# A stick-breaking attention stage: high parts of a head pair's result one step ahead of their low parts, and earlier requests for the second head's first queries

## The chip, the core and the metric

The kernel runs on one core of one Trainium2 chip. Its engines work side by side, each through its own instructions in program order: TensorE (PE: matrix products; its weight loads are listed as PEld), VectorE (DVE), ScalarE (ACT), GpSimd (POOL), and SyncE (SP), which issues most of the transfers between memory (HBM) and the core's on-chip memory. The metric is the device time of one execution in microseconds (us), lower being better, as the median of several executions. A profile of one execution, taken apart from the timed ones, says when each instruction ran and what ended each engine's idle time.

## What is computed

One inference step of a one-layer streaming encoder on a prompt of 1024 frames, and on 32 sample frames behind a cache of 256. After a norm and one wide projection come three branches: attention with 8 heads of 64, a short convolution, and two gates. Then follow an output projection, a wide layer with a squared ReLU, an embedding branch and a final norm. The part around the change is the attention of the prompt:

```python
def stick_breaking(q, k, v, q_pos, k_pos):
    scale = 1.0 / math.sqrt(HEAD_DIM)
    z = jnp.einsum('bqhd,bkhd->bhqk', q.astype(jnp.float32), k.astype(jnp.float32)) * scale
    mask = k_pos[None, :] < q_pos[:, None]
    log_1m = jnp.where(mask, jax.nn.log_sigmoid(-z), 0.0)
    tail = lax.cumsum(log_1m, axis=3, reverse=True) - log_1m
    a = jnp.where(mask, jnp.exp(jax.nn.log_sigmoid(z) + tail), 0.0)
    out = jnp.einsum('bhqk,bkhd->bqhd', a, v.astype(jnp.float32))
    return out.astype(v.dtype)

# in layer(), with attend = stick_breaking swept over blocks of 128 queries:
    y_attn = attend(q, k, v).reshape(b, t, SB_WIDTH) @ w_attn_out
    conv_out, new_buf = causal_conv(cc * cx, conv_buf, conv_w)
    y_conv = (cb * conv_out) @ w_conv_out
    merged = jax.nn.sigmoid(ga) * y_attn + jax.nn.sigmoid(gc) * y_conv
```

All tensors are float32. For the products a float32 operand is written as a high part of lower precision and a low part, the rest; ACT makes the high part (a copy with a cast), DVE subtracts it to get the low part, and PE multiplies high by high, high by low and low by high.

## The kernel before

The program is one list of instructions for each engine. For PE, ACT, DVE and POOL it is written out by hand (`manual_schedule`), in the order in which the code calls them; the order of SP's transfers is made from the program's order and what they depend on. Completed transfers are counted by eight counters used in turn, so that on SP a transfer also waits for the one that was issued eight before it.

The attention of the prompt is a loop over 64 steps `(p, j, i)`: 4 head pairs p, the 2 heads j of a pair, and 8 blocks i of 128 queries; step n = 16 p + 8 j + i. At loop turn n these things are issued, by the letters of `ORDER`:

- `scores` (S) for step n: PE multiplies the block's queries by the keys (`z`, lines L1421 and L1422), ACT takes the sigmoid (`r`, L1423), POOL masks the diagonal block (L1430).
- `weigh` (L) for step n-1: a scan on DVE along the keys (`r`, L1437), the running product of the sticks. Behind it `settle_owed` adds the two halves of an earlier product into the pair's result `oT` (L1408, a DVE addition).
- `flip` (A and B) for step n-2: PE turns the weights (`pa`, L1473), ACT makes their high part and DVE the low part (`at`, L1476 and L1477).
- `gather` (G) for step n-3, after every second block: PE multiplies the turned weights by the values (`av`, L1492), and ACT moves one half out (`avl`, L1503).
- `fill` (F), between these: products of other stages, of the embedding (`ps_pw`) first and of the convolution branch (`ps_oc`) later, which keep PE busy.

Queries come in pieces of two blocks: `queries(p, j, c)` asks for one of four pieces of a head in three transfers (128, 64 and 64 KB, lines L1384 to L1386) into one of three buffers `Q`. The four pieces of the very first head have their own buffers and are asked for earlier. From turn 4 on, at each even turn, the piece of step n+4 is asked for. Keys and values of a head (`ks`, L1391, and `vv`, L1393) are asked for eight steps ahead, at the third block of the head before. Other transfers of that time are the sample's cache (`cv<-in_cache_v_dram`), an output of the embedding (`ed<-em`, 528 KB) and operands of the convolution.

When a head pair is done, `oT[p]` (128 x 1056) is split into `oh[p]` and `ol[p]` for the branch's output product. `branch_parts(p, c)` does half c of it: c=0 at the end of turn 16 (p+1) + 8, c=1 one turn later (`BP = (8, 9)`), that is at turns 24 and 25, 40 and 41, 56 and 57 for pairs 0 to 2, and after the loop for pair 3. Through `split_into` (L1509 and L1510) it issues the copy on ACT (`o0h` and so on) and at once the subtraction on DVE (`o0l`).

Of the kernel before, what the change touches and what calls it, by code (L numbers as in the profile page):

```python
# [9 lines left out]
F32 = mybir.dt.float32  # L10
# [65 lines left out]
def tile_step(  # L76
# [8 lines left out]
    nc = tc.nc  # L85
# [7 lines left out]
    def blk(name, dt=F32, shape=None):  # L93
        return bpool.tile(shape or [P, T], dt, tag="B", name=name)
# [55 lines left out]
    halves = [slice(0, TH), slice(TH, T)]  # L150
    quarters = [slice(t * TQ, (t + 1) * TQ) for t in range(4)]
    oper = {k: [None] * 4 for k in ("B11", "B12", "B21", "B22", "T1", "T2", "T3", "T4")}
    add, sub = ALU.add, ALU.subtract
    dve, pool = nc.vector.tensor_tensor, nc.gpsimd.tensor_tensor
# [876 lines left out]
    oT = []  # L1031
# [345 lines left out]
    def queries(p, j, c):  # L1377
        if (p, j) == (0, 0):
            q = blk(f"q{c}", F32R, [P, 2, 256])
        else:  # L1380
            q = apool.tile([P, 2, 256], F32R, tag="Q", name=f"q{p}{j}{c}", bufs=3)
        live["q", p, j, c] = q
        src = qd[p, 64 * j : 64 * j + 64, :, c * 256 : (c + 1) * 256]
        nc.sync.dma_start(q[0:64, :, :].bitcast(F32), src)  # L1384
        nc.sync.dma_start(q[64:128, 0, :].bitcast(F32), src[:, 1, :])
        nc.sync.dma_start(q[64:128, 1, :].bitcast(F32), src[:, 0, :])  # L1386

    def keys_values(p, j):
        kk = st["k", p, j] = blk(f"ks{p}{j}", F32R, [P, SEQ])
        for i in range(2):  # L1390
            nc.sync.dma_start(kk[64 * i : 64 * i + 64, :].bitcast(F32), kd[p, i, 64 * j : 64 * j + 64, :])  # L1391
        vv = st["v", p, j] = blk(f"vv{p}{j}", F32R, [P, 8, P])
        nc.sync.dma_start(vv.bitcast(F32).rearrange("p a c -> p (a c)"), vd[p, j])  # L1393

    def branch_parts(p, c):
        if c == 0:
            oh.append(blk(f"o{p}h", F32R))  # L1400
            ol.append(blk(f"o{p}l", F32R))
        split_into(oh[p], ol[p], oT[p], [halves[c]])

    owed = []

    def settle_owed():
        while owed:
            owed.pop(0)()  # L1408

    steps = [(p, j, i) for p in range(4) for j in range(2) for i in range(8)]  # L1410

    def scores(p, j, i):
        q, kk = live["q", p, j, i // 2], st["k", p, j]
        L = P * (i + 1)
        nh = 1 if L <= 512 else 2
        W = L // nh
        tq = slice((i % 2) * P, (i % 2) * P + P)
        r = apool.tile([P, SEQ], F32, tag="R", name=f"r{p}{j}{i}", bufs=4)
        for h in range(nh):
            z, c = zps.tile([P, 512], F32, tag="z", name=f"z{p}{j}{i}{h}")[:, :W], slice(h * W, h * W + W)  # L1420
            nc.tensor.matmul(z, q[:, 0, tq], kk[:, c], start=True, stop=False)  # L1421
            nc.tensor.matmul(z, q[:, 1, tq], kk[:, c], start=False, stop=True)  # L1422
            nc.scalar.activation(r[:, c], z, AF.Sigmoid, scale=-1.0)  # L1423
        earlier(r[:, L - P : L], 1.0)
        live[p, j, i] = (r, L)
# [18 lines left out]
    def weigh(p, j, i):  # L1444
        left_over(*live[p, j, i])
# [6 lines left out]
    def flip(p, j, i):  # L1452
        nm = f"{p}{j}{i}"
        s, L = live.pop((p, j, i))
        c, u = i // 2, i % 2
        if u == 0:
            live["A"] = [[None, None], [None, None]]
            for s_ in range(2):
                nblk = min(4, 2 * c + 2 - 4 * s_)
                if nblk <= 0:  # L1460
                    continue
                for hl in range(2):
                    if nblk == 4:
                        a = blk(f"at{nm}{hl}{s_}", F32R, [P, 4, 256])
                    else:
                        a = apool.tile([P, 2, 256], F32R, tag="A2", name=f"at{nm}{hl}{s_}", bufs=2)
                    live["A"][hl][s_] = a
        A = live["A"]
        for b0 in range(0, i + 1, 4):
            nb = min(4, i + 1 - b0)  # L1470
            pt = turned([P, 4, P], f"pa{nm}{b0}")
            for b in range(nb):
                nc.tensor.transpose(pt[:, b, :], s[:, (b0 + b) * P : (b0 + b + 1) * P], ident)  # L1473
            ah = A[0][b0 // 4][:, :nb, u * P : (u + 1) * P]
            al = A[1][b0 // 4][:, :nb, u * P : (u + 1) * P]
            nc.scalar.copy(ah, pt[:, :nb, :])  # L1476
            nc.vector.tensor_tensor(al, pt[:, :nb, :], ah.bitcast(F32), op=ALU.subtract)  # L1477
            if b0 == 0 and i >= 4:
                yield
        if u:  # L1480
            live["A", p, j, c] = A

    def gather(p, j, c):
        A = live.pop(("A", p, j, c))
        vv = st["v", p, j]
        av = turned([P, 256], f"av{p}{j}{c}")
        n = 2 * c + 2
        turns = [(b, hl) for b in range(n - 2) for hl in range(2)]
        turns += [(n - 2, 0), (n - 1, 0), (n - 1, 1), (n - 2, 1)]
        for k, (b, hl) in enumerate(turns):  # L1490
            q0 = P * (b == n - 1)
            nc.tensor.matmul(  # L1492
                av[:, q0:], vv[:, b, :], A[hl][b // 4][:, b % 4, q0:],
                start=k == 0, stop=k + 1 == len(turns),
            )
        if j == 0 and c == 0:
            oT.append(blk(f"oT{p}"))
        if j == 1 and c == 3:
            nc.scalar.copy(oT[p][:, SEQ:], osT[:, p, :])
        lo = tpool.tile([64, 256], F32, tag="avl", name=f"avl{p}{j}{c}", bufs=2)  # L1500
        for u in range(2):
            q = slice(u * P, u * P + P)
            nc.scalar.activation(lo[:, q], av[0:64, q], AF.Identity, bias=vend[:, p, 8 * j + 2 * c + u : 8 * j + 2 * c + u + 1])  # L1503
        owed.append(partial(dve, oT[p][64 * j : 64 * j + 64, c * 256 : (c + 1) * 256], av[64:128, :], lo, op=add))


    def split_into(h, l, src, parts):
        for c in parts:
            nc.scalar.copy(h[:, c], src[:, c])  # L1509
            nc.vector.tensor_tensor(l[:, c], src[:, c], h[:, c].bitcast(F32), op=ALU.subtract)  # L1510
# [8 lines left out]
    oh, ol, mg, mh, ml = [], [], [], [], []  # L1519
# [26 lines left out]
    def gates_load(n):  # L1546
        sg = merge_gates[n] = [blk(f"s{n}{i}") for i in range(2)]
        for i in range(2):
            nc.sync.dma_start(sg[i], gd[8 * i + n])

    def gates_ready(n):
        if n < RAW_GATES:
            sg = merge_gates[n][0]
            scaled(sg)
            nc.scalar.activation(sg, sg, AF.Sigmoid)
# [35 lines left out]
    def fill(upto):  # L1591

        nonlocal done
        while done < upto - 0.1:
            done += next(work, 1.0)
# [136 lines left out]
    with tc.manual_schedule(engines=MM):  # L1732
        next(sample)
        for n in range(len(steps) + LAG + 1):
            done_f, parts = 0, None
            w0, w1 = (pace_ + [FILL])[n : n + 2]
            if n < len(steps):
                i = steps[n][2]
                if i % 2 == 0 and 4 <= n < len(steps) - 4:
                    p_, j_, i_ = steps[n + 4]  # L1740
                    queries(p_, j_, i_ // 2)
                if i == 2 and n + 8 < len(steps):
                    keys_values(*steps[n + 8][:2])
            if n - 4 in (4, 6, 8, 11, 12, 13, 14):
                next(sample)

            for op in ORDER:
                if op == "S" and n < len(steps):
                    scores(*steps[n])
                elif op == "L":  # L1750
                    if 1 <= n <= len(steps):
                        weigh(*steps[n - 1])
                    settle_owed()
                elif op == "F":
                    done_f += 1
                    fill(START + w0 + (w1 - w0) * done_f / nf)
                elif op == "G" and n > LAG and steps[n - LAG - 1][2] % 2 == 1:
                    p, j, i_ = steps[n - LAG - 1]
                    gather(p, j, i_ // 2)
                elif op in "AB" and LAG <= n < len(steps) + LAG:  # L1760
                    if op == "A":
                        parts = flip(*steps[n - LAG])
                    next(parts, None)
            if n in range(*AT):
                next(sums_w, None)
            if 16 < n < 64 and n % 16 in BP:
                branch_parts(n // 16 - 1, BP.index(n % 16))
        settle_owed()
        branch_parts(3, 0)
        branch_parts(3, 1)  # L1770
        gates_load(0)
        gates_ready(0)
    c_att.close()
# [1017 lines left out]
```

## Time and profile before

| | us |
|---|---|
| median of 3 runs | 1508.69 |
| lowest and highest of them | 1507.28, 1509.08 |
| the profiled execution | 1510.69 |
| its span on the core | 1508.8 |

How to read the rows that follow. A row of the timeline gives start, duration, engine, line, operation, out<-in, shape and count; idle time of the engine ahead of it stands in brackets, with what ended it. SPq is the issuing of a transfer on SP's queue, not its way through the DMA engines; the list of transfers gives KB of one and us from issue to landing. A row of the list of waits gives the total, how often, and the longest. A row of a window gives its length, the busy time of PE, PEld, DVE, ACT and POOL with counts, then the granted clock of PE, the busy share of the DMA engines and their GB/s. Starts of matrix products are recorded, their ends are modelled.

### The profile page before, as it was taken

The numbers are of one execution on the slowest core, as the hardware profiler recorded it, in microseconds if no ns is written. First come the engines' busy times: TensorE is split into PE (matmuls) and PEld (weight loads), VectorE is DVE, ScalarE is ACT, GpSimd is POOL, SyncE is SP. The second block draws the span as 40 slices with busy tenths as digits, with TensorE's granted clock in tenths as the row PEclk, the third lists the DMA queues.
The fourth block names the chain that finished last, engine by engine and source line by source line (L and its number), as shares of the span: only waits on it lengthen the run. The fifth ranks groups of instructions, "written<-read, shape, count | busy, mean of one in ns | idle before, by whom it ended". The sixth has DMA issues, their size and how long they took to land.

```text
span 1508.8 us, 29621 instructions
## 1 busy us (share of the span) xinstructions
PE 1491.1 (99%) x11520; PEld 1476.0 (98%) x11520; DVE 1189.2 (79%) x1716; ACT 802.7 (53%) x1595; POOL 376.8 (25%) x326
## 2 busy tenths in 40 slices
PE   9999999999999999999999999999999999999997
PEld 9999999999999999999999999999999999999997
DVE  6867788879578999876788778888688878879766
ACT  7654444445467767433475555555655433334655
POOL 0434334444121222003323344344000000000251
PEclk9999999999999999999999999999999999999999
DMA  6624425422679666654647677766989757855443
GB/s 242 215 72 170 169 58 198 156 84 92 225 244 278 182 167 140 225 199 160 230 175 245 242 258 250 253 240 226 352 300 287 245 190 244 286 185 167 141 128 123
DMA packets 127773, 303.37 MB, mean 201 GB/s; under 512 B 14961, under 2 KB 35569, under 8 KB 127633
## 3 DMA queue, kind: packets, MB, share of 16 engines
q1 hardware_dynamic: 122512, 286.97, 56.1%
q0 software_dynamic: 1728, 6.29, 2.5%
q10 hardware_dynamic: 3392, 8.23, 1.6%
q8 instruction: 90, 1.47, 0.4%
q14 instruction: 51, 0.41, 0.1%
HBM read 219.89 MB, written 89.93 MB: 205 GB/s over the span
## 4 chain that ended last, share of the span: by engine, by line
PE 86%; DVE 6%; DMA 3%; ACT 3%; issue 1%; SPq 0%; ACTq 0%; DVEq 0%
PE ps_dn L2220 6%; PE ps_dn L2218 6%; PE ps_dn L2219 6%; PE ps_A11i L453 4%; PE ps_A11i L454 4%; PE ps_A11i L455 4%; PE ps_A11u L453 3%; PE ps_A11u L454 2%; PE ps_A11u L455 2%; PE av L1492 2%; PE ps_wo L133 2%; PE ps_wo L135 2%; PE ps_wo L134 2%; PE ps_S1i L455 2%; PE ps_S1i L454 2%; PE ps_S1i L453 2%
## 5 line engine op out<-in xcount | busy, mean ns | idle before, releaser
L2220 PE MATMUL ps_dn<-fhP,wlo_dn 128*128 128x264 f32 x768 | 218.5, 285 | 0.0
L2218 PE MATMUL ps_dn<-fhP,whi_dn 128*128 128x264 f32 x768 | 218.3, 284 | 0.0
L2219 PE MATMUL ps_dn<-flP,whi_dn 128*128 128x264 f32 x768 | 218.2, 284 | 0.0
L2220 PEld LDWEIGHTS ps_dn<-fhP,wlo_dn 128*128 128x128 f32 x768 | 144.5, 188 | 0.0
L2218 PEld LDWEIGHTS ps_dn<-fhP,whi_dn 128*128 128x128 f32 x768 | 144.5, 188 | 0.0
L2219 PEld LDWEIGHTS ps_dn<-flP,whi_dn 128*128 128x128 f32 x768 | 144.4, 188 | 0.0
L2433 POOL TENSOR_TENSOR xx<-xx,pgs 128x400 f32<-128x400 f32 (+1 forms) x17 | 20.1, 1184 | 280.3 <-DVE pgs L2432 279.8
L1437 DVE TENSOR_TENSOR_SCAN r<-r 128x128 f32<-128x128 f32 (+3 forms) x64 | 86.7, 1355 | 4.1 <-POOL r L1430 4.1
L453 PE MATMUL ps_A11i<-T,shS_i 128*128 128x264 f32 x288 | 82.4, 286 | 0.7 <-ACT u_i L596 0.7
L454 PE MATMUL ps_A11i<-T,shS_i 128*128 128x264 f32 x288 | 82.2, 285 | 0.0
L455 PE MATMUL ps_A11i<-T,slS_i 128*128 128x264 f32 x288 | 82.0, 285 | 0.0
L453 PE MATMUL ps_A11u<-T,shS_u 128*128 128x264 f32 x256 | 73.2, 286 | 2.5 <-ACT u_u L596 2.5
L454 PE MATMUL ps_A11u<-T,shS_u 128*128 128x264 f32 x256 | 72.8, 285 | 0.0
L455 PE MATMUL ps_A11u<-T,slS_u 128*128 128x264 f32 x256 | 72.8, 284 | 0.0
L1430 POOL TENSOR_SCALAR_AFFINE_SELECT r<-r 128x128 f32<-128x128 f32 x64 | 35.3, 551 | 134.2 <-ACT r L1423 134.1
L2062 ACT CAST whi_dn<-raw_dn 128x1024 fp32r<-128x1024 f32 x31 | 32.6, 1053 | 65.5 <-PE ps_dn L2219 50.1
L2084 DVE TENSOR_TENSOR flP<-mrP,fhP 128x1056 fp32r<-128x1056 f32 x48 | 60.1, 1253 | 6.3 <-ACT fhP L2079 6.3
L135 PE MATMUL ps_wo<-mh,wlo_wo 128*128 128x352 f32 x192 | 62.0, 323 | 0.0
L134 PE MATMUL ps_wo<-ml,whi_wo 128*128 128x352 f32 x192 | 61.9, 322 | 0.0
L133 PE MATMUL ps_wo<-mh,whi_wo 128*128 128x352 f32 x192 | 61.6, 323 | 0.0
L1477 DVE TENSOR_TENSOR at<-pa,at 128x512 fp32r<-128x512 f32 (+2 forms) x96 | 50.7, 549 | 11.5 <-ACT at L1476 10.6
L251 DVE TENSOR_TENSOR slS_i<-s_i,shS_i 128x512 fp32r<-128x512 f32 x54 | 48.2, 893 | 13.1 <-ACT shS_i L191 12.9
(2058 smaller groups left out, 5831.3 us busy)
## 6 DMA issues: line engine op xcount, KB each, us to landing
raw_dn<-in_w_down_dram SPq DMA_DIRECT2D x59, 512.0 KB, 5.1
mrP<-mdT SPq DMA_DIRECT2D x32, 528.0 KB, 5.6
mdB<-m SPq DMA_DIRECT2D x48, 264.0 KB, 2.6
ztT<-zduT SPq DMA_DIRECT2D x24, 528.0 KB, 4.9
mrP<-mdB SPq DMA_DIRECT2D x24, 528.0 KB, 7.3
ztB<-zduB SPq DMA_DIRECT2D x18, 528.0 KB, 4.7
s<-gd SPq DMA_DIRECT2D x16, 528.0 KB, 5.2
mdT<-ta SPq DMA_DIRECT2D x32, 264.0 KB, 2.3
```

The lines of the kernel that those rows point to most:

```text
L133: nc.tensor.matmul(ps, wh, xh[k][:, cols], start=(k == order[0]), stop=False)
L134: nc.tensor.matmul(ps, wh, xl[k][:, cols], start=False, stop=False)
L135: nc.tensor.matmul(ps, wl, xh[k][:, cols], start=False, stop=(k == order[-1]))
L453: nc.tensor.matmul(p_, wh[:, k, :], h, start=new and n == 0, stop=False, **on)
L454: nc.tensor.matmul(p_, wh[:, k, :], l, start=False, stop=False, **on)
L455: nc.tensor.matmul(p_, wl[:, k, :], h, start=False, stop=z, **on)
L1437: nc.vector.tensor_tensor_scan(rev, rev, rev, 1.0, ALU.mult, ALU.bypass)
L1477: nc.vector.tensor_tensor(al, pt[:, :nb, :], ah.bitcast(F32), op=ALU.subtract)
L2084: dve(l, mraw.pop(v), opd[v].bitcast(F32), op=sub)
L2218: nc.tensor.matmul(ps, hi[:, j, :], oh, start=j == 0, stop=False)
L2219: nc.tensor.matmul(ps, hi[:, j, :], ol, start=False, stop=False)
L2220: nc.tensor.matmul(ps, lo[:, j, :], oh, start=False, stop=j == NP_ - 1)
```

## The change

It has two parts. `branch_parts` now issues only the copy on ACT; the subtraction is kept in a list `parts_owed` and issued at the end of the next turn, ahead of that turn's own `branch_parts`. After the loop, the list is emptied in order. And the turn at which a piece of queries is asked for gets a lead from a small table: the piece of step 8 at turn 0 instead of 4, of step 10 at turn 2 instead of 6, of step 12 at turn 6 instead of 8; all others as before, four steps ahead.

```diff
+    parts_owed = []
+
     def branch_parts(p, c):
         if c == 0:
             oh.append(blk(f"o{p}h", F32R))
             ol.append(blk(f"o{p}l", F32R))
-        split_into(oh[p], ol[p], oT[p], [halves[c]])
+        nc.scalar.copy(oh[p][:, halves[c]], oT[p][:, halves[c]])
+        parts_owed.append(partial(dve, ol[p][:, halves[c]], oT[p][:, halves[c]], oh[p][:, halves[c]].bitcast(F32), op=sub))
...
                 i = steps[n][2]
-                if i % 2 == 0 and 4 <= n < len(steps) - 4:
-                    p_, j_, i_ = steps[n + 4]
+                lead = {0: 8, 2: 8, 4: 0, 6: 6, 8: 0}.get(n, 4)
+                if i % 2 == 0 and lead and n + lead < len(steps):
+                    p_, j_, i_ = steps[n + lead]
                     queries(p_, j_, i_ // 2)
...
             if n in range(*AT):
                 next(sums_w, None)
+            while parts_owed:
+                parts_owed.pop()()
             if 16 < n < 64 and n % 16 in BP:
                 branch_parts(n // 16 - 1, BP.index(n % 16))
         settle_owed()
         branch_parts(3, 0)
         branch_parts(3, 1)
+        while parts_owed:
+            parts_owed.pop(0)()
```

The order on PE, ACT and POOL is the same as before; only DVE and SP differ. On SP's queue, from the sample's values (`cv`) on, before (q_5659 is the piece of step 8, of which the 64x2x256 transfer stands further up in both; q_5723 is that of step 10, q_5810 of step 12; ks and vv are the keys and values of step 8's head):

```order
L1661 DMA cv<-in_cache_v_dram 128x1024
L1354 DMA ed<-em_5516 128x1056
L1391 DMA ks_5608<-kd 64x1024 x2
L1393 DMA vv_5611<-vd 128x1024
L1354 DMA ed<-em_5599 128x1056
L1385 DMA q_5659<-qd 64x256
L1386 DMA q_5659<-qd 64x256
L1384 DMA q_5723<-qd 64x2x256
L1385 DMA q_5723<-qd 64x256
L1386 DMA q_5723<-qd 64x256
```

And the same place of the changed program (step 8 is q_5565, step 10 q_5612, step 12 q_5727):

```order
L1664 DMA cv<-in_cache_v_dram 128x1024
L1385 DMA q_5565<-qd 64x256
L1386 DMA q_5565<-qd 64x256
L1354 DMA ed<-em_5516 128x1056
L1384 DMA q_5612<-qd 64x2x256
L1385 DMA q_5612<-qd 64x256
L1386 DMA q_5612<-qd 64x256
L1391 DMA ks_5616<-kd 64x1024 x2
L1393 DMA vv_5619<-vd 128x1024
L1354 DMA ed<-em_5603 128x1056
L1384 DMA q_5727<-qd 64x2x256
```

The queries of steps 8 and 10 have moved from behind the keys and values to ahead of them; between `cv` and the second half of the keys there are now seven transfers instead of two, so that this half is the eighth behind `cv`.

On DVE, turns 24 to 26 before (the scan stands here as SCALAR_TENSOR_TENSOR; r_6616 is step 24, r_6677 step 25, r_6721 step 26; at_6625 and at_6627 are the low parts of step 23's turned weights):

```order
L1477 TENSOR_TENSOR at_6627<-pa_6642,at_6626 128x3x128
L1510 TENSOR_TENSOR o0l<-oT_5689,o0h 128x528
L1437 SCALAR_TENSOR_TENSOR r_6616<-r_6616 128x128
L1408 TENSOR_TENSOR oT_6489<-av_6655,avl_6668 64x256
L1477 TENSOR_TENSOR at_6625<-pa_6685,at_6624 128x4x128
L1477 TENSOR_TENSOR at_6627<-pa_6702,at_6626 128x4x128
L1510 TENSOR_TENSOR o0l<-oT_5689,o0h 128x528
L1437 SCALAR_TENSOR_TENSOR r_6677<-r_6677 128x256
L1477 TENSOR_TENSOR at_6730<-pa_6731,at_6729 128x128
L1437 SCALAR_TENSOR_TENSOR r_6721<-r_6721 128x384
```

The same rows of the changed program (L1771 is the emptying of `parts_owed`):

```order
L1480 TENSOR_TENSOR at_6627<-pa_6642,at_6626 128x3x128
L1440 SCALAR_TENSOR_TENSOR r_6616<-r_6616 128x128
L1411 TENSOR_TENSOR oT_6489<-av_6655,avl_6668 64x256
L1480 TENSOR_TENSOR at_6625<-pa_6684,at_6624 128x4x128
L1480 TENSOR_TENSOR at_6627<-pa_6701,at_6626 128x4x128
L1771 TENSOR_TENSOR o0l<-oT_5693,o0h 128x528
L1440 SCALAR_TENSOR_TENSOR r_6676<-r_6676 128x256
L1480 TENSOR_TENSOR at_6729<-pa_6730,at_6728 128x128
L1771 TENSOR_TENSOR o0l<-oT_5693,o0h 128x528
L1440 SCALAR_TENSOR_TENSOR r_6720<-r_6720 128x384
```

Each of the two subtractions has gone down by one turn: the first from ahead of step 24's scan to behind step 23's weights, the second from ahead of step 25's scan to ahead of step 26's. The same happens at turns 40 to 42 and 56 to 58.

## The prediction

> **What bounds the kernel now.** I read the page first, for the engine that sets the end, then the list of what that engine waits for, then the order of time around each wait that the change can reach.
>
> ```profile
> span 1508.8 us, 29621 instructions
> PE 1491.1 (99%) x11520; PEld 1476.0 (98%) x11520; DVE 1189.2 (79%) x1716; ACT 802.7 (53%) x1595; POOL 376.8 (25%) x326
> PE 86%; DVE 6%; DMA 3%; ACT 3%; issue 1%; SPq 0%; ACTq 0%; DVEq 0%
> ```
>
> TensorE (PE) is busy for 99% of the span and carries 86% of the chain that ended last. No matmul is added or removed, and PE's order stays as it was, so the change can only win or lose time in which PE stands still. The list of PE's waits (total, times, longest) names those in the attention loop:
>
> ```profile
> PE z L1421 <- DMA q<-qd: 1.1, 1, 1.1
> PE av L1492 <- DVE at L1477: 0.8, 3, 0.3
> PE av L1492 <- DVE oT L1408: 0.3, 2, 0.2
> PE av L1492 <- ACT o1h L1509: 0.2, 1, 0.2
> ```
>
> One wait for queries, 1.1 us, and 0.8 + 0.3 + 0.2 = 1.3 us before the products `av`. The first is what the earlier requests are near; the second lies where `branch_parts` puts its work. The two are separate terms.
>
> **Term 1: the queries of the second head.** In the order of time PE stands before the scores of step 8, the first of head j=1:
>
> ```profile
> 442.31 1.08 PE L1668 MATMUL zs<-kk,qs 64*32 64x288 f32 x16
> 444.53 0.30 PE L1421 MATMUL z<-ks,q 128*128 128x128 f32 x1 [1.14 <-DMA q<-qd]
> ```
>
> PE was free at 443.39 and started at 444.53. What landed when is read from the chain (a piece from issue or previous landing to landing) and from the issues on SP's queue:
>
> ```profile
> 433.04 8.10 DMA ks<-kd
> 441.16 3.39 DMA q<-qd
> ...
> 430.50 1.03 SPq L1661 DMA_DIRECT2D cv<-in_cache_v_dram  x1
> 432.51 1.93 SPq L1391 DMA_DIRECT2D ks<-kd  x2
> 435.77 0.45 SPq L1385 DMA_DIRECT2D q<-qd  x1
> 436.26 0.89 SPq L1386 DMA_DIRECT2D q<-qd  x1
> 437.31 1.24 SPq L1384 DMA_DIRECT2D q<-qd  x1
> ```
>
> The keys of step 8 landed at 433.04 + 8.10 = 441.14. Two pieces of its queries were issued only at 435.77 and 436.26, behind keys, values and an output, and ended PE's wait at about 444.5. The DMA engines had no room in between:
>
> ```profile
> 430.00:442.00 12.00, 12.00 (x83) 11.42 (x82) 10.62 (x13) 10.17 (x27) 3.99 (x7) 1.00 1.01 334
> cv<-in_cache_v_dram SPq DMA_DIRECT2D x1, 512.0 KB, 6.8
> ks<-kd SPq DMA_DIRECT2D x2, 256.0 KB, 8.0
> ```
>
> Over these 12 us (the window's last two numbers) their share is 1.01 at 334 GB/s. A transfer is late by what stands ahead of it. In the changed order five more query pieces stand ahead of the keys: 64 KB + 64 KB of step 8 and 128 + 64 + 64 KB of step 10, by the shapes in SP's rows, together 384 KB or 393 kB. At 334 GB/s that is 1.2 us, so the keys land at 441.14 + 1.2 = 442.3 (an estimate from these rows). PE needs them at 443.39, so 1.0 us is to spare, and the queries are then long there. The step-10 queries, needed several steps later, buy nothing themselves. They are part of the load ahead of the keys.
>
> There is an added wait on SP's queue. The row at 437.31 starts just when `cv` has landed (430.50 + 6.8 = 437.30), eight transfers behind it; the same spacing of eight puts the second half of the keys at that place now. It is issued at about 437.3 instead of 433, with the values and the next output behind it. I take this as free, because about 1.2 MB (two query pieces, one 528 KB output, step 10's queries, the first half of the keys) is then still queued ahead of it, some 3.5 us at 334 GB/s. The bounds: the keys land no earlier than the 441.14 of now (gain 1.14 us, since PE is free at 443.39), and at the latest, with the 8.1 us that they took this time counted from 437.3, at 445.4, which makes PE wait 2.0 us and loses 0.9. I take **+1.1 us**, since the byte count is nearest to how the landings of now follow each other.
>
> The Trainium skill, "DMA: Bandwidth & Descriptors", section "Queues, rings and completion order", says that each DMA engine consumes the descriptors of a ring in order. By that rule this part speaks against itself, since earlier queries make the keys later, and it is what the rivals about the keys below live on. The landings of now agree: 64 KB pieces issued at 435.77 landed only after the 512 KB issued ahead of them.
>
> **Term 2: low parts one step later.** The place is step 26 (and 42 and 58, one for each head pair). PE, from the second score product (z) to the next one's first, at step 26 and, for comparison, at step 50, which has the same sequence without any `branch_parts`:
>
> ```profile
> 499.64 0.34 PE L1422 MATMUL z<-ks,q 128*128 128x384 f32 x1
> 500.49 0.35 PE L1492 MATMUL av<-at,vv 128*128 128x256 f32 x1 [0.16 <-DVE oT L1408]
> 501.12 2.04 PE L1492 MATMUL av<-at,vv 128*128 128x256 f32 x15 [0.28 <-DVE at L1477]
> 502.99 0.40 PE L1421 MATMUL z<-ks,q 128*128 128x512 f32 x1
> ...
> 564.98 0.34 PE L1422 MATMUL z<-ks,q 128*128 128x384 f32 x1
> 567.13 0.39 PE L1421 MATMUL z<-ks,q 128*128 128x512 f32 x1
> ```
>
> Step 26 takes 502.99 - 499.64 = 3.35 us, step 50 takes 567.13 - 564.98 = 2.15 us. The stretch loses 1.20 us, though the idle marks in it add up to 0.16 + 0.28 = 0.44 only. The Trainium skill, "Perfetto Trace Analysis", section "Identifying the Most-Contended Engine", warns that a busy TensorE is a poor measure because its instructions are pipelined. The two distances agree with it here: by the marks the three places would give 1.3 us, by starts up to 3.6. I count by starts.
>
> Who is late is seen on VectorE (DVE) and ScalarE (ACT) at step 25:
>
> ```profile
> 498.75 0.71 DVE L1510 TENSOR_TENSOR o0l<-oT,o0h 128x528 fp32r<-128x528 f32 x1 [0.76 <-ACT o0h L1509]
> 499.38 0.51 DVE L1437 TENSOR_TENSOR_SCAN r<-r 128x128 f32<-128x128 f32 x1
> 499.92 0.43 DVE L1408 TENSOR_TENSOR oT<-av,avl 64x256 f32<-64x256 f32 x1
> 500.37 1.29 DVE L1477 TENSOR_TENSOR at<-pa,at 128x512 fp32r<-128x512 f32 x2
> ...
> 497.58 0.61 ACT L1503 ACTIVATE avl<-av,vend 64x128 f32<-64x128 f32 x2 [0.95 <-PE av L1492]
> 498.09 0.62 ACT L1509 CAST o0h<-oT 128x528 fp32r<-128x528 f32 x1
> 498.89 0.57 ACT L1476 CAST at<-pa 128x512 fp32r<-128x512 f32 x1
> ...
> 494.25 0.55 POOL L1430 TENSOR_SCALAR_AFFINE_SELECT r<-r 128x128 f32<-128x128 f32 x1 [1.57 <-ACT r L1423]
> ```
>
> DVE stands 0.76 us idle for the high part, makes the low part, and has scan, `oT` and `at` queued behind it. Without it, DVE is free at 498.75 - 0.76 = 497.99, the scan's input was ready at 494.80, `oT`'s at 498.19, so both are over by about 498.7. Late next is the cast of the weights on ACT, which ends at 498.89 + 0.57 = 499.46. With the 0.04 us that DVE took to start behind ACT (o0h ends at 498.71, o0l starts at 498.75), `at` starts at 499.50 instead of 500.37: 0.87 us sooner, and the waiting `av` with it. The high parts stay on ACT ahead of that cast, so not all of the 1.20 comes back. The other two places, same pair of rows:
>
> ```profile
> 543.45 1.29 DVE L1477 TENSOR_TENSOR at<-pa,at 128x512 fp32r<-128x512 f32 x2
> 585.88 1.29 DVE L1477 TENSOR_TENSOR at<-pa,at 128x512 fp32r<-128x512 f32 x2
> ...
> 541.96 1.05 ACT L1476 CAST at<-pa 128x512 fp32r<-128x512 f32 x2
> 584.40 0.57 ACT L1476 CAST at<-pa 128x512 fp32r<-128x512 f32 x1
> ```
>
> 541.96 + 0.57 + 0.04 = 542.57 against 543.45, 0.88; 584.97 + 0.04 = 585.01 against 585.88, 0.87. The sum is 0.87 + 0.88 + 0.87 = 2.6 us; the bounds are 0 (another wait takes each place) and 3 x 1.20 = 3.6. I take 2.6, from the rows of the casts.
>
> What is moved comes back elsewhere: the first low part now stands behind `at` at the end of step 25, the second in front of the scan of step 26's keys. DVE's work of 0.71 us each is the same, but DVE meets the rest of the head with its old clock time while PE comes 0.87 us sooner. The tightest meeting I found is in the third pair:
>
> ```profile
> 595.50 1.75 DVE L1437 TENSOR_TENSOR_SCAN r<-r 128x768 f32<-128x768 f32 x1
> 597.78 0.60 PE L1473 MATMUL pa<-ident,r 128*128 128x128 f32 x4
> ```
>
> The scan ends at 597.25, 0.53 us ahead of the transposes that read it. PE gains 0.87 here, so up to 0.34 can be given back unless DVE uses its own idle time before. I take 0.2 for this, between 0 and 0.34. The last pair's low parts stand in the same place on DVE as before and cost nothing.
>
> **Sum.** 1.1 + 2.6 - 0.2 = 3.5 us. The profiled execution took 1510.69 us (span 1508.8), 2.0 above the median of the runs; its span becomes 1505.3. Taken from the median, 1508.69 - 3.5 = **1505.2 us**, -0.23%. About 0.2%, or 3.0 us, is what a measurement of this kernel can tell from no change, so the forecast lies just beyond it. Its own range is 1504 to 1506: up to 1.1 + 3.6 = 4.7 us of gain, down to 2.7.
>
> **Rivals.**
> - *DVE gives half of it back.* The moved parts lie in steps where DVE has little room, or PE pays only what its idle marks show. For it: DVE's scan only 0.53 us ahead above; marks of 0.44 at each place. Against it: the equal stretch at step 50 is 1.20 us shorter. It gives 1.1 + 1.3 = 2.4 us, 1506.3.
> - *The keys take the queries' place.* The second half of the keys lands at 445.4 as bounded above, so the first part doesn't do what it says: PE waits 2.0 us, now for keys. For it: the issue moves from 433 to 437.3 and transfers here took 8.0 us. Against it: what they waited for was the bytes ahead of them. It gives 2.4 - 0.9 = 1.5 us, 1507.2.
> - *Slower, by the same keys.* Place: the scores of step 8. Each later row of SP's queue waits in turn, and of the `cv` transfers from 425 to 450 us the slowest took 10.0 us:
>
> ```profile
> DMA to landing us min/median/max: 6.6/8.0/10.0
> ```
>
> Issued at 437.3 and 10.0 us on the way, the keys land at 447.3: 2.8 us later than PE starts now, and against 2.4 from the low parts 0.4 us is lost, 1509.1. It decides from a landing at 444.53 + 2.4 = 446.9 on. The bytes speak against it.
>
> **How the numbers follow.** Forecast 0.62, half given back 0.20, keys in the queries' place 0.11, slower 0.07. The predicted time is the forecast's, 1505.2. The range reaches from the forecast's upper bound of gain (4.7 us, 1504.0, and 0.3 of scatter) to 1507.5, past the second rival's 1507.2; it leaves out the slower case and what lies beyond these bounds. Faster by over 0.2% needs 3.0 us, which most of the forecast's range and nothing else gives: 0.53. Slower by over 0.2% needs a landing still later than the one worked out: 0.04. Within 0.2%: 0.43.
>
> **What the profile will show.** Right: no wait of PE for `q` near 443, step 8's scores 1.1 us sooner against the products `zs`; the stretch z to z of steps 26, 42 and 58 at about 2.5 us instead of 3.35; no idle DVE ahead of `o0l`. Wrong: a wait of `z` on `ks` near 443; `at` still after 500 at step 26, relative to the score product; new waits of `pa` on DVE's scans in the steps behind.

## The result, and the profile after

| | us |
|---|---|
| kernel before, 13 runs: median (lowest to highest) | 1508.94 (1507.28 to 1510.84) |
| changed kernel, 13 runs: median (lowest to highest) | 1506.72 (1505.16 to 1509.26) |
| ratio, with its 95% interval | 0.9985 (0.9978 to 0.9992) |
| the profiled execution of the changed kernel, its span | 1505.48, 1503.8 |

The change wins 0.15%: 2.2 us between the medians, 1.2 to 3.3 by the interval. The forecast was 3.5. The two profiled executions differ by 1510.69 - 1505.48 = 5.2 us, because that of before lay near the top of its runs and that of after near the bottom. So the difference of the two spans is no measure of the change; the places are.

The page after shows the same work, and a chain on which PE's share has risen:

```profile
span 1503.8 us, 29621 instructions
PE 1491.1 (99%) x11520; PEld 1477.0 (98%) x11520; DVE 1188.7 (79%) x1716; ACT 802.8 (53%) x1595; POOL 382.2 (25%) x326
PE 93%; DVE 3%; ACT 1%; DMA 1%; issue 1%; ACTq 0%; DVEq 0%; SPq 0%
```

The list of PE's waits after is (engine, line, releaser: total, times, longest, in us):

```profile
PE ps_A11u L453 <- ACT u_u L596: 1.4, 1, 1.4
PE ps_idle L1610 <- DVE eps_t L104: 1.1, 1, 1.1
PE ps_oa L135 <- DVE wlo_oa L125: 1.0, 2, 0.7
PE ps_f L1238 <- ACT xs L1234: 0.5, 1, 0.5
PE z L1424 <- ACT r L1426: 0.4, 2, 0.2
```

Of the four rows that the prediction showed, none is left: no wait of `z` for `q`, and none of `av`. In the order of time, PE after, first at step 8 and then at step 26 (which now stands 2.17 us earlier in its span):

```profile
442.75 1.07 PE L1671 MATMUL zs<-kk,qs 64*32 64x288 f32 x16
443.75 0.33 PE L1424 MATMUL z<-ks,q 128*128 128x128 f32 x1
...
498.33 0.34 PE L1425 MATMUL z<-ks,q 128*128 128x384 f32 x1
498.53 2.45 PE L1495 MATMUL av<-at,vv 128*128 128x256 f32 x16
500.82 0.39 PE L1424 MATMUL z<-ks,q 128*128 128x512 f32 x1
...
540.51 0.34 PE L1425 MATMUL z<-ks,q 128*128 128x384 f32 x1
542.97 0.39 PE L1424 MATMUL z<-ks,q 128*128 128x512 f32 x1
...
582.11 0.34 PE L1425 MATMUL z<-ks,q 128*128 128x384 f32 x1
584.60 0.39 PE L1424 MATMUL z<-ks,q 128*128 128x512 f32 x1
```

Step 8's scores follow the products `zs` by 443.75 - 442.75 = 1.00 us, where it was 444.53 - 442.31 = 2.22. The score-to-score stretches are 2.49, 2.46 and 2.49 us. Before they were 3.35 (502.99 - 499.64), 3.35 (546.06 - 542.71) and 3.34 (588.49 - 585.15), so each place gains 0.85 to 0.89. The `av` products run as one piece of 16. The engines behind step 25 show why:

```profile
498.20 1.47 DVE L1480 TENSOR_TENSOR at<-pa,at 128x512 fp32r<-128x512 f32 x2 [0.71 <-ACT at L1479]
499.58 0.70 DVE L1771 TENSOR_TENSOR o0l<-oT,o0h 128x528 fp32r<-128x528 f32 x1
...
497.59 0.57 ACT L1479 CAST at<-pa 128x512 fp32r<-128x512 f32 x1
```

The cast on ACT ends at 497.59 + 0.57 = 498.16, and `at` starts 0.04 us behind it. ACT's cast is late next, as the prediction had it, and DVE now waits 0.71 us for that cast instead of 0.76 for the high part.

What is lost again lies behind the third pair, in steps 58 to 63. DVE's rows there, before:

```profile
590.08 0.42 DVE L1477 TENSOR_TENSOR at<-pa,at 128x256 fp32r<-128x256 f32 x1 [0.18 <-ACT at L1476]
...
591.80 0.56 DVE L1477 TENSOR_TENSOR at<-pa,at 128x384 fp32r<-128x384 f32 x1 [0.17 <-ACT at L1476]
...
601.99 2.28 DVE L1437 TENSOR_TENSOR_SCAN r<-r 128x1024 f32<-128x1024 f32 x1
```

and after, from the two subtractions on:

```profile
583.41 0.70 DVE L1771 TENSOR_TENSOR o2l<-oT,o2h 128x528 fp32r<-128x528 f32 x1
...
584.91 0.69 DVE L1771 TENSOR_TENSOR o2l<-oT,o2h 128x528 fp32r<-128x528 f32 x1
585.52 0.94 DVE L1440 TENSOR_TENSOR_SCAN r<-r 128x384 f32<-128x384 f32 x1
...
586.95 0.42 DVE L1480 TENSOR_TENSOR at<-pa,at 128x256 fp32r<-128x256 f32 x1
...
588.43 0.53 DVE L1480 TENSOR_TENSOR at<-pa,at 128x384 fp32r<-128x384 f32 x1
...
598.54 2.28 DVE L1440 TENSOR_TENSOR_SCAN r<-r 128x1024 f32<-128x1024 f32 x1
...
603.64 0.69 DVE L1480 TENSOR_TENSOR at<-pa,at 128x512 fp32r<-128x512 f32 x1 [0.59 <-ACT at L1479]
```

The two short idle times of before (0.18 and 0.17) are used up, and DVE runs without a marked gap until the one of 0.59 in the last row. The kernel before has no marked gap there either from 591.80 on, so what DVE lags by then it can't make up. PE around this stretch: the score that ends step 58's stretch (after, the row at 584.60 above), a group of eight `av` products with the score behind it, and the first output product, after and then before:

```profile
591.96 1.32 PE L1495 MATMUL av<-at,vv 128*128 128x256 f32 x8
593.12 0.39 PE L1424 MATMUL z<-ks,q 128*128 128x512 f32 x1
...
606.64 0.32 PE L133 MATMUL ps_oa<-o0h,whi_oa 128*128 128x352 f32 x1
```

```profile
588.49 0.39 PE L1421 MATMUL z<-ks,q 128*128 128x512 f32 x1
...
595.84 1.17 PE L1492 MATMUL av<-at,vv 128*128 128x256 f32 x8
596.85 0.39 PE L1421 MATMUL z<-ks,q 128*128 128x512 f32 x1
...
610.12 0.32 PE L133 MATMUL ps_oa<-o0h,whi_oa 128*128 128x352 f32 x1
```

At step 58 PE is 588.49 - 584.60 = 3.89 us ahead of its old time, but DVE's long scan behind it is only 601.99 - 598.54 = 3.45 us ahead, and PE's first output product 610.12 - 606.64 = 3.48 us. So 3.89 - 3.48 = 0.41 us of the gain is gone by then, where 0.2 was forecast. It goes at three places, none of which carries an idle mark: 0.15 at the `av` products shown (from their start to the next score 593.12 - 591.96 = 1.16 us against 596.85 - 595.84 = 1.01), 0.06 at a group of transposes `pa` 4.5 us behind their start, and 0.19 at the next `av` products. The eight `av` products shown read a low part that DVE finished at 594.89 + 0.69 = 595.58 before, only 0.26 us ahead of them.

### The profile page after: what moved, and what is told of

Same layout as the page of the kernel before. It is cut to its first block, busy times and chain, and to the rows that moved or that the text cites. A ratio compares the mean times of both kernels' runs of the same rounds, so it can differ in the third digit from the quotient of the medians.

```text
span 1503.8 us, 29621 instructions
## 1 busy us (share of the span) xinstructions
PE 1491.1 (99%) x11520; PEld 1477.0 (98%) x11520; DVE 1188.7 (79%) x1716; ACT 802.8 (53%) x1595; POOL 382.2 (25%) x326
## 4 chain that ended last, share of the span: by engine, by line
PE 93%; DVE 3%; ACT 1%; DMA 1%; issue 1%; ACTq 0%; DVEq 0%; SPq 0%
PE ps_dn L2226 6%; PE ps_dn L2228 6%; PE ps_dn L2227 6%; PE ps_A11i L454 5%; PE ps_A11i L453 5%; PE ps_A11i L455 5%; PE ps_A11u L453 3%; PE ps_A11u L454 3%; PE ps_A11u L455 3%; PE av L1495 3%; PE ps_S1i L454 2%; PE ps_S1i L455 2%; PE ps_S1i L453 2%; PE ps_wo L135 2%; PE ps_wo L133 2%; PE ps_wo L134 2%
## 5 line engine op out<-in xcount | busy, mean ns | idle before, releaser
L1433 POOL TENSOR_SCALAR_AFFINE_SELECT r<-r 128x128 f32<-128x128 f32 x64 | 39.6, 619 | 125.8 <-ACT r L1426 125.8
```

## The experiments

By places, the changed kernel should gain more than 2.2 us, and the question was where the rest went. The texts name theories by letters. A: both parts act in full, and the rest is scatter. B (B1 in one of the texts): the wait for queries comes and goes between executions, with how fast the transfers ahead of them run. B2: moving the low parts takes that wait away as well. C: gain is given back behind the attention. D: DVE, crowded by the moved parts, gives it back. The distances below are between starts of PE's rows: "zs to z" from step 15's `zs` to step 8's first score, "z to z" the three stretches, "58 to output" from the score that ends the third stretch to the first output product.

**One part at a time.** First the earlier requests alone (the kernel before with the new lead table):

```diff
-                if i % 2 == 0 and 4 <= n < len(steps) - 4:
-                    p_, j_, i_ = steps[n + 4]
+                lead = {0: 8, 2: 8, 4: 0, 6: 6, 8: 0}.get(n, 4)
+                if i % 2 == 0 and lead and n + lead < len(steps):
+                    p_, j_, i_ = steps[n + lead]
```

> Only the table of leads is in; the low parts stay where they were. Distances are read between starts on PE: from the sample's scores (zs) to step 8's scores, 2.22 us before and 1.00 after the change; from the second score product to the next step's first at steps 26, 42 and 58, 3.35 us before, 2.46 to 2.49 after; from the first score product to the first product of the attention's output (ps_oa), 183.65 before, 179.73 after. Theory A (the two parts act each in its own place, in every execution, and what the median lacks against the profile is scatter of other stages): zs to step 8 at 1.0, the three places still 3.35, the stage 182.0 to 182.5, the time 1.2 to 1.7 us under before, ratio 0.9990. Theory B (the wait for the queries was large in the one profiled execution of before and is small in most): the same distances in this profile, but the time within 0.5 us of before. Theory C (the gain is given back behind the attention): the stage shorter as under A, and the rest of the program longer by about 1 us in every profile.

Measured: 1508.44 us, ratio 0.9995 (0.9986 to 1.0004). At its place the part does what it says, 1.01 from zs to z. The stretches are as before, here the first of them:

```profile
443.51 1.08 PE L1668 MATMUL zs<-kk,qs 64*32 64x288 f32 x16
444.52 0.33 PE L1421 MATMUL z<-ks,q 128*128 128x128 f32 x1
...
499.08 0.34 PE L1422 MATMUL z<-ks,q 128*128 128x384 f32 x1
...
502.45 0.40 PE L1421 MATMUL z<-ks,q 128*128 128x512 f32 x1
```

502.45 - 499.08 = 3.37 us. So the two parts touch different places. The timed gain is about 0.75 us by the ratio and nothing by the medians (1508.42 in the runs of the kernel before beside it). The interval takes in both no gain and the 1.1 us that was forecast, so this run alone doesn't decide between A and B.

Then the low parts alone (the changed kernel with the old rule for the requests), twice:

```diff
-                lead = {0: 8, 2: 8, 4: 0, 6: 6, 8: 0}.get(n, 4)
-                if i % 2 == 0 and lead and n + lead < len(steps):
-                    p_, j_, i_ = steps[n + lead]
+                if i % 2 == 0 and 4 <= n < len(steps) - 4:
+                    p_, j_, i_ = steps[n + 4]
```

> Only the low parts are moved; the queries are asked for as before. Theory A: the three places at 2.5 us, zs to step 8 near 2.2, the stage at 181.3 to 181.7 (3 x 0.87 less the 0.4 given back behind the third place), the time 2.2 us under before, ratio 0.9985. Theory B: the same, and the time equals that of the whole change, since the leads bring nothing in most executions. Theory C: the stage shorter by 2.2, the time by about 1.

> The low parts alone once more. In its first profile PE did not wait for the queries (zs to step 8's scores 1.01 us) though they were asked for as before; in both profiles of before it waited (2.22 and 2.18). Theory B1 (the wait for the queries comes and goes between executions, with how fast the transfers ahead of them ran: the sample's values landed after 6.6 to 6.8 us where PE waited, after 4.6 to 5.7 where it did not): either 1.0 or about 2.2 us, and the queries' landing tells which. Theory B2 (moving the low parts takes the wait away in some way of its own): 1.0 again with the transfers as slow as before. The three places 2.5 in both.

Measured: 1506.01 us, ratio 0.9987 (0.9979 to 0.9996), and 1507.30, ratio 0.9988 (0.9978 to 0.9998). Nearly the whole gain is here. The surprise is step 8, here of the first of the two:

```profile
442.27 1.08 PE L1671 MATMUL zs<-kk,qs 64*32 64x288 f32 x16
443.27 0.33 PE L1424 MATMUL z<-ks,q 128*128 128x128 f32 x1
```

PE doesn't wait for the queries, though they are asked for as late as before. The second execution shows the same distance, 1.01. The keys ahead of them, two transfers of 256 KB, were faster on their way:

```profile
DMA to landing us min/median/max: 6.4/6.7/7.0
```

The changed kernel and the kernel before were run again beside them, unaltered.

> The changed kernel once more, for a second profile and a second measurement. Theory A: zs to step 8 at 1.0, the three places at 2.5, the stage at 179.7 within 0.3, and a time 3.0 to 3.8 us under before, ratio 0.9975 to 0.9980. Theory B: the time about 2.2 under before, as first measured. Theory C: the stage at 179.7, but the time 2.2 under before and the rest longer than before's 843.45 us from the output projection on.

> The kernel before once more, to see what its profile shows a second time and how far two measurements of one program lie apart. Theory A: zs to step 8 at 2.0 to 2.4, the three places at 3.35, the stage at 183.7 within 0.3, ratio 1.000 within 0.0006. Theory B: zs to step 8 clearly under 2, near 1.2, the stage near 182.7. Theory C: as A, and 843.4 us from the output projection on.

Measured: the changed kernel 1506.25 us, ratio 0.9988 (0.9979 to 0.9997); the kernel before against itself 1508.73, ratio 1.0003 (0.9994 to 1.0011). In the latter the wait is there again:

```profile
441.84 1.08 PE L1668 MATMUL zs<-kk,qs 64*32 64x288 f32 x16
444.01 0.30 PE L1421 MATMUL z<-ks,q 128*128 128x128 f32 x1 [1.10 <-DMA q<-qd]
```

and the keys took longer:

```profile
DMA to landing us min/median/max: 7.8/8.1/8.3
```

Two profiles with the old low parts have the wait and two with the moved ones don't; B had expected near 1.2 us from zs to z in this second profile of the kernel before, and it is 2.17. So B2 explains these four as well as B. Two things speak against B2. The two programs issue the transfers of this stretch in the same order on SP, and the first subtraction that moves runs at 498.75 us in the kernel before, 54 us behind step 8. And if the low parts brought 1.1 us more than the 2.2 of their places (2.6 less 0.4), they would win 3.3 us. The mean of the 19 runs of the two low-part kernels is 1506.87, that of the 52 runs of the kernel before beside them 1508.78, a gain of 1.9.

**More bytes ahead of the queries.** To tell B from B2, a second load of the cached values (512 KB, read by nothing) was put behind the first:

```diff
         nc.sync.dma_start(cv, cache_v)
+        nc.sync.dma_start(blk("cv2", F32, [P, 2, SB]), cache_v)
```

First one execution of each, with the low parts alone and with the whole change:

> The low parts alone, with one more transfer of 512 KB (the sample's values a second time, into a tile that nobody reads) ahead of step 8's keys and queries. If bytes ahead make the wait, 512 KB at 334 GB/s put the queries 1.6 us later: zs to step 8's scores at 2.6 to 3.8 us, PE waiting on q. If the wait has to do with something else (the issue of the queries, a buffer), it stays between 1.0 and 2.2 us.

> The whole change with the same 512 KB more ahead. By the prediction's count the keys have 1.0 us to spare in the changed order, so 1.6 us of bytes leave PE waiting 0.6 us, on the keys and not on the queries: zs to step 8's scores at 1.4 to 1.8 us, that is 1.0 to 2.0 us less than with the low parts alone under the same load. If the earlier requests only exchange the queries for the keys, both kernels wait alike under this load.

Measured: 1511.45 and 1505.92 us, one run each. The low parts alone, then the whole change:

```profile
444.52 1.08 PE L1672 MATMUL zs<-kk,qs 64*32 64x288 f32 x16
447.54 0.30 PE L1424 MATMUL z<-ks,q 128*128 128x128 f32 x1 [1.94 <-DMA q<-qd]
```

```profile
442.56 1.07 PE L1672 MATMUL zs<-kk,qs 64*32 64x288 f32 x16
444.06 0.30 PE L1424 MATMUL z<-ks,q 128*128 128x128 f32 x1 [0.42 <-DMA vv<-vd]
```

The wait for queries is there with the low parts moved, 1.94 us, so B2 falls. The earlier requests take it away. In its place comes 0.42 us, which the profile puts down to the values of the second head. But the scores don't read the values, which were issued at 438.3 and took 6.6 us, to 444.9, when the scores had begun. The second half of the keys was issued at 437.8 and landed 5.9 to 6.1 us later, by 443.7 to 443.9, so the keys are what PE most likely waited for: the second rival of the prediction, at a fifth of its 2.0 us, and only under this load.

Then the same load timed, with the kernel before as well:

> The kernel before, with one more 512 KB load of the cached values put on SP's queue right behind the one that is there (its result is read by nothing). Theory B (the wait for step 8's queries is real, and its size goes with how fast the transfers ahead of them run): from the start of step 15's score block to step 8's first score about 3.0 us in the profile, as in the same load with the low parts alone moved (3.02), against 2.2 in the kernel before; the three score-to-score stretches 3.35 each; time about 0.8 us above the kernel before, so near 1509.5. Rival (the wait is an effect of one execution, and timed runs don't show it): time equal to the kernel before within 0.3 us.

> Low parts moved, queries asked for as before, one more 512 KB load behind the cached values; timed this time. Theory B: 3.0 us from step 15's score block to step 8's first score, the wait for q about 1.9; score-to-score 2.48 at the three places; the time is 2.0 us under the kernel before with the same load (three times 0.87, less 0.6 given back behind), so near 1507.5. Rival: no wait in timed runs, 1506.7 like the low parts alone.

> The whole change with one more 512 KB load behind the cached values; timed. Theory B: 1.5 us from step 15's score block to step 8's first score (0.4 of it a wait for the keys, which now come behind the queries), so 1.5 us less than with the low parts alone under this load: near 1506.0, ratio to the kernel before 0.9982. Rival (queries asked for sooner are worth nothing in timed runs): the same time as the low parts alone under this load, within 0.3 us.

| with the extra load | median us | ratio to the kernel before without it | zs to z | wait for `q` |
|---|---|---|---|---|
| kernel before | 1509.27 | 1.0006 (0.9997 to 1.0015) | 2.11 | 1.03 |
| low parts alone | 1508.14 | 0.9999 (0.9990 to 1.0009) | 1.93 | 0.84 |
| whole change | 1506.29 | 0.9986 (0.9977 to 0.9995) | 1.01 | none |

The 3.0 us from zs to z that was expected of the first two did not come again: it was 1.94 of waiting in one execution and 0.84 in another of the same program. But the timed difference did come: with this load the earlier requests are worth 1508.14 - 1506.29 = 1.85 us (1.5 expected; the two intervals overlap a little), and the whole change 2.98 us. The rival by which earlier queries bring nothing to timed runs falls, for this load. In this execution of the whole change the 0.42 us didn't come again (1.01 from zs to z). One expectation of this set failed: the low parts alone were to win 2.0 us against the kernel before under the same load, and won 1509.27 - 1508.14 = 1.13. So part of the 1.85 us may be the scatter of that run.

All executions with the requests as before, by the time that the pair of keys took from issue to landing:

| kernel | extra load | low parts moved | keys, us to landing | wait for `q`, us |
|---|---|---|---|---|
| low parts alone | no | yes | 6.4 to 7.0 | none |
| low parts alone, again | no | yes | 7.0 to 7.8 | none |
| low parts alone | yes | yes | 7.4 to 7.9 | 0.84 |
| before | yes | no | 7.5 to 8.1 | 1.03 |
| before | no | no | 7.8 to 8.1 | 1.14 |
| before, again | no | no | 7.8 to 8.3 | 1.10 |
| low parts alone | yes | yes | 8.4 to 9.1 | 1.94 |

The wait grows with the keys' time, nearly row by row, and within the low-parts program alone from none to 1.94 us. The bytes moved say the same: over the 8 us ahead of `zs` the DMA engines moved 352 and 348 GB/s in the two executions without the wait and 307 to 330 GB/s in the five with it. No execution of the kernel before without the wait was profiled, so that some of its timed runs lack it is inferred. What decides the speed isn't shown by these runs.

**The give-back.** If DVE's lack of a gap behind step 58 is what gives back, it should shrink when DVE has less to do there. POOL was given the low parts, first of all four pairs:

```diff
-        parts_owed.append(partial(dve, ol[p][:, halves[c]], oT[p][:, halves[c]], oh[p][:, halves[c]].bitcast(F32), op=sub))
+        parts_owed.append(partial(pool, ol[p][:, halves[c]], oT[p][:, halves[c]], oh[p][:, halves[c]].bitcast(F32), op=sub))
```

> The whole change, with the moved low parts subtracted on GpSimd instead of VectorE. Behind step 58 the attention takes 22.05 us to the first output product (ps_oa) in the three profiles with moved low parts and 21.62 to 21.68 without. Theory D (VectorE is too full behind the moved parts, which gives 0.4 us back): 21.6 to 21.7 now, the stage 0.4 us shorter, the time 0.3 to 0.5 us under that of the change, which the timing can hardly tell. Rival E (what comes back is due to ScalarE or to PE's place in the loop): 22.05 as it is. Rival F (a subtraction on GpSimd is so long that the masks behind it come late): new waits of PE for weights at steps 26 to 28, the stage longer by 0.5 to 3 us.

then of the first three alone (`partial(pool if p < 3 else dve, ...)`):

> The whole change, the low parts of the first three pairs computed by POOL in place of DVE, the last pair's by DVE as they are. If what is given back behind the third pair comes from DVE, which runs there without a gap: step 58's first score to the output projection 21.90 us (21.62 in the kernel before, 22.05 in the changed one), and from there to the next projection 48.0 as in the changed kernel, not the 48.48 of POOL computing the last pair's too. A scan of DVE beside a low part of POOL takes about 2.07 us where it took 0.95, so most of what DVE is freed of comes back. Time 0.15 us under the changed kernel: 1506.4, ratio 0.9985; if the 1505.3 of all four pairs on POOL was more than scatter, 1504.8 (0.9975).

Measured: 1505.25 us, ratio 0.9978 (0.9968 to 0.9988), and 1505.14, ratio 0.9977 (0.9969 to 0.9986). POOL and DVE of the first of them, at the third pair, and PE where the attention ends:

```profile
583.35 1.32 POOL L1771 TENSOR_TENSOR o2l<-oT,o2h 128x528 fp32r<-128x528 f32 x1
...
583.41 2.07 DVE L1440 TENSOR_TENSOR_SCAN r<-r 128x384 f32<-128x384 f32 x1
...
597.56 2.28 DVE L1440 TENSOR_TENSOR_SCAN r<-r 128x1024 f32<-128x1024 f32 x1
...
583.79 0.39 PE L1424 MATMUL z<-ks,q 128*128 128x512 f32 x1
...
605.69 0.32 PE L133 MATMUL ps_oa<-o0h,whi_oa 128*128 128x352 f32 x1
```

DVE is freed of 0.70 + 0.69 = 1.39 us, but its scan takes 2.07 us beside POOL's subtraction where it took 0.94 alone, so about 0.3 us of work is gone. The Trainium skill, "SBUF — State Buffer", section "SBUF: two separate sides", describes the ports that DVE and GpSimd share as an exclusive lock, held by whichever instruction starts first until it ends; on DVE's side it names instructions with two inputs from SBUF, and this scan reads `r` as both of its inputs. This row agrees: POOL starts 0.06 us ahead and the scan grows by 1.13, most of POOL's 1.32.

From 58 to the output it is 605.69 - 583.79 = 21.90 us, against 610.12 - 588.49 = 21.63 in the kernel before and 606.64 - 584.60 = 22.04 in the changed one. With three pairs on POOL it is 607.03 - 585.15 = 21.88:

```profile
585.15 0.39 PE L1424 MATMUL z<-ks,q 128*128 128x512 f32 x1
...
607.03 0.32 PE L133 MATMUL ps_oa<-o0h,whi_oa 128*128 128x352 f32 x1
```

So about 0.15 of the 0.41 us comes back, where D had said all of it (21.6 to 21.7) and E none (22.05); the new waits of F aren't there, the three stretches being 2.47 to 2.49 us. The size missed because the longer scan takes most of what DVE is freed of. That DVE is the cause is seen when its lag is measured like PE's, from the score that ends step 58's stretch to DVE's long scan: 601.99 - 588.49 = 13.50 us before, 598.54 - 584.60 = 13.94 in the changed kernel, and 597.56 - 583.79 = 13.77 with POOL. DVE lags 0.44 and 0.27 us behind its old place, and PE has lost 0.41 and 0.27 by the output. With three pairs on POOL it is 0.26 (a scan at 598.91) and 0.25. PE's loss is DVE's lag each time.

These two are the fastest kernels of the study: the 20 runs have a mean of 1505.35 us, the 24 runs of the changed kernel 1506.77, though they weren't timed side by side. Of these 1.4 us the attention shows about 0.3: from its first score to the first output product it is 179.5 us in both, and 179.7 and 179.9 in the two profiles of the changed kernel. Where the rest is from isn't settled, since the stretches ahead of and behind the attention differ by up to 2.5 and 1.6 us between two executions of one and the same kernel. Behind the attention the last pair went as expected: from the first output product to the next projection it is 48.0 us when DVE computes it and 48.5 when POOL does.

## Why the prediction was right, and where it was off

1506.72 lies in the stated range, and within 0.2% of the kernel before, to which the prediction gave 0.43, against 0.53 for faster by more than that. It does not lie in the forecast's own range, 1504 to 1506: the lower end of gain there, 2.7 us, was worked out from no row, and it is the widening to 1507.5 for the rival of the keys that takes the result in. That rival didn't come up, so this part was luck. The forecast of 1505.2 was 1.5 us too fast. By its steps:

- **Term 2, +2.6 us: right, mechanism and size.** The three stretches got shorter by 0.86 + 0.89 + 0.85 = 2.6 us, with the cast on ACT late next. Counting by starts was right: the idle marks of before added up to 1.3. One small sum in it is off: from 497.99 the scan (0.51) and `oT` (0.43) end at 498.93, not at 498.7, which is still ahead of the cast's 499.46, so nothing hangs on it.
- **The give-back, -0.2 us: the mechanism right, the place and the size wrong.** It is 0.41 up to the first output product. The working took a scan and the transposes behind it, 0.53 us apart, for the tightest meeting and bounded the loss by it. DVE comes 0.44 us late (3.89 - 3.45), so that meeting costs nothing: the transposes stand about 0.15 us late, as the scores ahead of them do. PE loses its time at others, first at the `av` products with 0.26 us of room. As DVE has no marked gap from 583.41 to 603.05 to catch up in, PE ends up behind by nearly all of DVE's lag. With it, the low parts alone give 2.6 - 0.4 = 2.2 at their places, and 1.9 was timed.
- **Term 1, +1.1 us: the mechanism right, the size wrong.** This is the term that was mis-sized. Each changed profile without extra load has PE at step 8 with no wait to speak of, so the wait of the profile before does go. But the sum took a wait of one execution for one of all, and subtracted it from the median of runs. Two of four executions with the old requests and no extra load had none to lose, both of them with the low parts moved. Timed alone it brought 0.05% (0.75 us, and by its interval anything from none to 2.1), and beside the low parts nothing that can be told: 0.9985 and 0.9988 with both parts, 0.9987 and 0.9988 without this one, and means of 1506.77 (24 runs) and 1506.87 us (19 runs). Only with 512 KB more ahead did it show in the timed runs, as 1.85 us.
- **The sum.** 2.6 - 0.4 + (0 to 0.75) = 2.2 to 3.0, against 2.2 (1.2 to 3.3) measured.
- **The keys, said to land with 1.0 us to spare.** They did better. In the changed kernel the pair was issued nearly as late as was said, and took less time on its way, 5.2 us at most. The rows of the tile `ks` (first and last start of its issues, and the time to landing):

```profile
L1391 SPq DMA_DIRECT2D ks<-kd x2: 594/594/595, 436.1 to 436.8; - x2
...
DMA to landing us min/median/max: 4.7/5.0/5.2
```

Issued last at 436.8 they had landed by 442.0, and PE needed them at 443.75. Taking the later issue as free was right: the keys were issued 3.6 to 3.8 us later and landed less than 1 us later than the 441.14 of before. Neither rival on the keys came up, but for the 0.42 us under extra load, in one of two executions.
- **The rival "DVE gives half of it back"** has the nearest time (1506.3), but for the wrong reason: DVE gave back 0.4 of 2.6, and most of the rest of the shortfall is Term 1, as far as timed runs can tell.

## What to carry to other kernels

A wait for a transfer that one profile shows may not be there in the next execution of the same program (with the extra load, the whole change waited 0.42 us in one and not at all in the other); look at it in several profiles before its length goes into a sum, while a wait between engines that a fixed order sets repeats to some hundredths (here the stretch of 3.35 us in every profile without the moved parts, 3.34 to 3.39). When PE gains time at one place, compare the starts of the helper engine's long instructions behind it: if that engine runs there without a gap, PE keeps only what the helper gained. Earlier requests can be worth having as cover, even where they don't shift the median: with 512 KB more ahead, the kernel that had them stayed at 1506.3 us, the one without went to 1508.1.

## What the runs showed of the hardware

- The same two transfers of 256 KB, behind the same transfers, took 6.4 to 7.0 us to land in one execution (low parts alone) and 7.8 to 8.3 in another (the kernel before), on a queue that kept the DMA engines busy (share 1.00 from 430 to 442 us in both). PE's wait for what follows them was none in the one and 1.10 us in the other.
- Transfers issued later took less: the keys landed 4.7 to 5.2 us after an issue at 436.1 and 7.8 to 8.1 us after one at 432.5, so that the landing moved by less than the issue did.
- 512 KB more on the queue did not lengthen the wait in a regular way: 0.84 and 1.94 us in two executions of one program.
- A DVE scan beside a POOL subtraction took 2.07 us in place of 0.94, so that handing POOL 1.39 us of DVE's work freed DVE by 0.3 and brought its later work forward by less than 0.2.
